# Buffers on multiples of 512 bytes, and half of the later weight buffers 256 bytes off

## The chip, the cores and the metric

The kernel runs on one core of a Trainium2 chip. The metric is the device time of one execution in microseconds, the median of several runs. A core has TensorE for matrix products (each a load of a stationary operand of up to 128 columns, and the streaming of a moving operand of up to 512), VectorE, ScalarE and GpSimd for elementwise work, and queues that start DMAs; on-chip memory has 128 partitions, and "bytes" below are bytes within a partition.

## What is computed

Two blocks, one after the other, on 512 tokens of 1024 features in float32:

```python
def reference(x, ...):
    # first block: h = rmsnorm(x); proj = h @ w_in; three mixers; w_out; residual; gated feed-forward
    x = first_block(x, ...)
    # second block, two layers: even_mixer or odd_mixer, then a feed-forward with a causal convolution
    return second_block(x, ...)

def first_block(...):
    ...
    mix = jnp.concatenate([att, ssd, gdn], axis=-1) @ w_out[l]
    x = x + rmsnorm(mix, post_mix_norm[l])
    h = rmsnorm(x, pre_ffn_norm[l])
    f = (jax.nn.silu(h @ ffn_w_gate[l]) * (h @ ffn_w_up[l])) @ ffn_w_down[l]
    x = x + rmsnorm(f, post_ffn_norm[l])

def second_block(...):
    for layer in range(DEPTH_2):
        m = even_mixer(...) if layer % 2 == 0 else odd_mixer(...)
        x = layer_norm(ALPHA * x + m, ln_g[layer, 0], ln_b[layer, 0])
        f = conv_ffn(x, ffn_w_up[layer], ffn_conv_w[layer], ffn_w_down[layer])
        x = layer_norm(ALPHA * x + f, ln_g[layer, 1], ln_b[layer, 1])
```

The feed-forwards are 2816 wide. Most of the arithmetic is in the products with weights: the projections of three mixers, their output products, and three feed-forwards.

## The kernel before

Products with weights are done to nearly float32 precision from parts: each operand is split exactly into a high and a low part (`split`, lines 327 to 330: ScalarE casts to the high part, VectorE subtracts for the low part; float32r is the type of the parts), and three products are summed in one PSUM bank, high with high, high with low, low with high.

There are two forms. `fm` (lines 350 to 352) makes a block of 128 output features for all tokens: the weights (128 columns, 512 bytes) are loaded, and the activations (512 tokens, 2048 bytes) are the moving operand; eight k-tiles of three products are 24 matmuls. `fm_first` (line 354) does the first blocks behind a tail in two halves of 256 tokens. `tm_k` (lines 364 to 366), called from `tm`, from `out_proj` and from `down` in `ffn`, makes a token tile: the activations (128 tokens, 512 bytes) are loaded and the weights (192 to 512 columns) are the moving operand.

The phases run one after the other: `block1_mix`, output product (`wo1`), feed-forward (`wf1`), `even_mix`, `wo2`, `wf2`, `odd_mix`, `wo3`, `wf3`. A feed-forward makes 11 hidden tiles (22 blocks of `fm`), multiplies them down (`down`), makes 11 more, multiplies seven down, and does the last four token tile by token tile with the tail (`Tail`: residual, norms, transposes, the next operand).

Weights come through `Stream.next` (line 224): 128 x 1024 floats from SyncE's queue into a raw buffer, split into a high and a low one. The pool `const` has two raw buffers and three of each part; between `wo1` and `wf1`, and again from `wo2` to the end, a second pool `w` of the same size is open (`more_weights`), and buffers are taken from the two in turn. The activations of products have two homes: A (`half_act("A")`, in the pool `const`) holds a mixer's output, a feed-forward's hidden tiles 0 to 7 of eleven and block 1's input; B (in the pool `x`, at the right end of the memory, with the residual stream) holds the input of the feed-forwards and of the later mixers. Hidden tiles 8 to 10 are in `hid`.

A pool gives its tiles addresses in the order of their first allocation, each rounded up to 32 bytes. `const` begins at 16,512 (a multiple of 512 and 128 more) with `cst` (5224 bytes), `vecs` (256), `rows` (2512), `eps6` and `eps5` (4 each); A, the raw buffers and the weight parts follow, all multiples of 4096. Pool `w` begins where `const` ends, the pool of a phase where `w` ends. `x` ends at 229,344 and is 49,152 bytes long. Adding up gives where the operands of the products begin, in bytes past a multiple of 512 (each later k-tile, half or token tile in them lies whole multiples of 512 further):

| operand | before | after |
|---|---|---|
| A | 32 | 0 |
| weights in `const` | 32 | 0 |
| weights in `w`, `wo1` and `wf1` | 32 | 0 |
| weights in `w`, `wo2` to `wf3` | 32 | 256 |
| B | 480 | 0 |
| `hid` in `wf1` | 160 | 0 |
| `hid` in `wf2` and `wf3` | 192 | 256 |

Two small tiles matter below: `strictr`, loaded by the products of L508 and L509 in block 1, and their moving operand `tda`, both at 352.

Of the kernel before, what the change touches and what calls it, by code (L numbers as in the profile page):

```python
# [26 lines left out]
# ---------------------------------------------------------------- host layout  # L27

def _fm(w, cols=None):
    """Columns in blocks of 128, each block as [k-row, k-tile, column]."""  # L30
    w = np.asarray(w)
    if cols is not None:
        out = np.zeros((w.shape[0], len(cols)), w.dtype)
        cols = np.asarray(cols)
        out[:, cols >= 0] = w[:, cols[cols >= 0]]
        w = out
    k, c = w.shape
    return w.reshape(k // 128, 128, c // 128, 128).transpose(1, 2, 0, 3).reshape(128, -1)


def _tm(w, cols=None, rows=None):
    """[k-row, k-tile, column] of a group of columns."""
    w = np.asarray(w)
    if cols is not None:
        w = w[:, np.asarray(cols)]
    if rows is not None:
        w = w[np.asarray(rows)]
    k, c = w.shape
    return w.reshape(k // 128, 128, c).transpose(1, 0, 2).reshape(128, -1)
# [18 lines left out]
def _vec(w):  # L68
    """[c] or [n, c] to [128, c/128 * n], channel on the partition."""
# [53 lines left out]
def _t5_onehot():  # L123
    """Column m holds the bucket of distance 255 - m."""
# [7 lines left out]
# packed rows that every partition holds  # L132
# [8 lines left out]
# packed vectors with the channel on the partition  # L141
# [7 lines left out]
# columns of w_in, and how its rows and those of w_out are placed  # L149
# [66 lines left out]
# ---------------------------------------------------------------- kernel  # L216

class Stream:
    """Weights in the order of their use: loaded ahead and split exactly, w = hi + lo. The buffers that stay for
    the whole kernel take turns with those of k.wpool, where that is open."""  # L220
# [4 lines left out]
    def next(self, n, tail=False):  # L225
        """tail: needed at the end of a tail, when VectorE is the busiest."""
# [14 lines left out]
class Kern:  # L241
    def __init__(self, tc, ctx, io):
# [9 lines left out]
        self.eps5 = self.cpool.tile([128, 1], F32, name="eps5")  # L252
        nc.gpsimd.memset(self.eps5, 1e-5)
        self.ident = self.c("ident")
        self.wpool, self.wturn = None, 0
        self.banks = ctx.enter_context(tc.tile_pool(name="banks", bufs=1, space=PSUM))

    def more_weights(self):
        """Further buffers for the weights, over several phases."""
# [14 lines left out]
    def rings(self, **r):  # L274
        """Rings of PSUM banks, for this phase."""
# [36 lines left out]
    # ---- the activations of the next product, feature on the partition, split as hi + lo  # L312

    def open_x(self, ctx):
        """The residual stream, and the second set of operands."""
# [3 lines left out]
    def half_act(self, which, g, dt=F32R):  # L319
        pool = self.cpool if which == "A" else self.xpool  # L320
        return tuple(pool.tile([128, 4, T], dt, name=f"act{p}{g}", bufs=1) for p in "hl")

    def new_act(self, which):
        """A mixer's output is in A, the residual stream as an operand in B (in A before the first mixer)."""
        return {g: self.half_act(which, g) for g in range(2)}

    def split(self, hi, lo, src, eng=None):
        """hi + lo = src, exactly."""
# [3 lines left out]
    def put_act(self, a, t, src, ring):  # L332
        """src: token tile t [128, D], token on the partition."""
# [11 lines left out]
    def fm(self, ps, w, act, nk=KD, s=slice(0, T)):  # L345
        """ps [128, T] = (block of 128 columns)^T act, for the tokens s."""
# [7 lines left out]
    def fm_first(self, ws, act, n, ring, tail):  # L354
        """The first n blocks after a tail: the first two token tiles of each, then the others."""
# [12 lines left out]
    def tm(self, w, act, n, ring, use, ts=range(NT)):  # L368
        """use(t, ps): token tile t of a group of n columns, token on the partition."""
# [8 lines left out]
    def rsqrt(self, out, ss, scale, eps, pool):  # L378
        """(ss * scale + eps) ** -0.5 by Newton's steps on VectorE (ScalarE's tables stay as they are)."""
# [14 lines left out]
def block1_mix(k):  # L394
    """Pre-norm, projections and the three mixers. Returns what w_out multiplies."""
# [3 lines left out]
    # what lives to the end  # L399
# [12 lines left out]
    # pre-norm  # L412
# [16 lines left out]
    def silu2(out, ps):  # L429
        """2 silu"""  # L430
# [3 lines left out]
    # ---- the small projections, attention's v, the delta rule's gate (token on the partition)  # L434
# [11 lines left out]
    def bc(ap, n):  # L446
        """[128, a, b] against [128, a, b, n]."""
# [5 lines left out]
    # gates: da = -exp(A_log) softplus(x + bias) for the four delta heads and the eight of the state space  # L453
# [46 lines left out]
    def decay_ps(mask, t, h0, tag):  # L500
        """[s, 4, t]: the sum of da over s < k <= t."""
# [10 lines left out]
    # the decays within the chunks: for the systems (strict, times -beta) and for the queries  # L512
# [12 lines left out]
    # ---- gated delta rule: q, k, v  # L525
# [4 lines left out]
    def conv(out, ps, wname, b, bias):  # L530
        """silu of the causal convolution of four taps over the tokens; the taps and the bias are halved,
        and silu(2 y) = y (1 + tanh(y))."""
# [23 lines left out]
    # normalised q, k  # L556
# [19 lines left out]
    def chunk_stage(t):  # L576
# [17 lines left out]
        for i, dst in enumerate((gA, gQK)):  # L594
# [4 lines left out]
            if i == 0:  # L599
                # the diagonal blocks of 16, by column  # L600
# [12 lines left out]
    # the unit triangular blocks of 16, one per partition: inverses by substitution  # L613
# [23 lines left out]
    # right-hand sides  # L637
# [9 lines left out]
    # ---- state space: B, C, x, then its gate  # L647
# [5 lines left out]
    # ---- banded attention with sinks  # L653
# [108 lines left out]
    # blocks of 16 to blocks of 32, then the solution of each chunk: above and below the diagonal block of 32  # L762
# [58 lines left out]
    # the chunks' maps of the state, S -> A S + B, and what the state gives to the outputs  # L821
# [27 lines left out]
    # the recurrence over chunks of 64 tokens; the states of two heads on the diagonal of one tile  # L849
# [40 lines left out]
    # what w_out multiplies: state space, delta rule, attention; the norms of the first three token tiles together  # L890
# [14 lines left out]
    for ts in (range(3), range(3, NT)):  # L905
# [6 lines left out]
        # of the doubled gates: half of them, over the root of a quarter of their mean square  # L912
# [11 lines left out]
def softplus(k, pool, out, x, bias, shape):  # L924
    """max(x, 0) + log1p(exp(-|x|)), of x + bias; log1p(e) = 2 atanh(e / (2 + e)) by its series."""
# [24 lines left out]
class Tail:  # L950
    """Residual and norms at the end of a branch, token tile by token tile, up to the next product's operand."""

    def __init__(self, k, pool, kind, i, j, ring):
        """kind "rms": x += rmsnorm(y) * gain i, then rmsnorm * gain j (None: x as it is);
        "ln": x = layernorm(y) * gain i + gain j, y with the residual already in it."""
# [7 lines left out]
    def table(self):  # L963
        """Sqrt's table, before it is waited for."""
# [10 lines left out]
    def part(self, t, c, ps, acc=None):  # L975
        """Half c of the branch's output for token tile t, or the first part of its sum."""
# [7 lines left out]
    def more(self, t, c, ps):  # L984
        """A further part of the sum."""
# [3 lines left out]
    def last(self, t, c, ps, more):  # L989
        """The last part of half c (or all of it), with its statistics."""  # L990
# [17 lines left out]
    def tile(self, t, out=None):  # L1008
        """The rest, once both halves are there."""
# [7 lines left out]
        else:  # L1017
            # minus the mean, then the squares of what is left
# [36 lines left out]
def out_proj(k, ws, act, tail, order):  # L1055
    """The product at the end of a mixer (eight k-tiles), with its tail. Rings "y" of four banks, "z" of two."""
# [26 lines left out]
def ffn(k, wname, act, cvec, kind, gi, gj, out=None):  # L1083
    """The gated feed-forward, plain or (cvec) with its causal convolution of three taps; its tail."""
# [3 lines left out]
    with tc.tile_pool(name=wname, bufs=1, reuse_waits="tile") as P:  # L1088
        k.rings(h=(0, 1, 2, 3), y=(4, 5, 6, 7), bt=(0, 1))
        ws = Stream(k, k.io[wname])  # L1090
        tail = Tail(k, P, kind, gi, gj, "bt")
        taps = None if cvec is None else k.load_vec(cvec, P)
        ha = k.new_act("A")
        hp = P.tile([128, 2, 3, T], F32R, name="hid", bufs=1)
# [60 lines left out]
def even_mix(k, act):  # L1155
    """The even mixer: indexed latent attention and forgetting attention."""
# [26 lines left out]
    # t5 bias of the tokens up to 255 behind a query, by head: a Toeplitz tile from a row, first upside down  # L1183
# [6 lines left out]
    brow = tile_([8, 384], "brow")  # L1190
# [7 lines left out]
    # the index: queries, key, head weights; the forget gates  # L1198
# [288 lines left out]
```

## Time and profile before

| | us |
|---|---|
| median of 3 runs | 1941.91 (1941.82 to 1942.63) |
| span of the profiled execution | 1938.9 |
| TensorE busy with matmuls | 1896.9 (98%) |
| TensorE's weight loads, beside the matmuls | 1554.8 (80%) |
| VectorE busy | 1068.7 (55%) |
| ScalarE busy | 726.9 (37%) |
| GpSimd busy | 158.2 (8%) |

The span runs from the first to the last instruction; the times of the runs contain what lies around it too. Matmuls overlap in the profile, and their ends are modelled; the distance from the start of one to the start of the next is what one costs in a dense stretch. The rows come from the page of the profile, the chain of work that ended last, the waits of TensorE, the groups of instructions by shape, the windows (busy time, count of instructions, granted clock of a stretch) and the timeline (instructions in order of time).

### The profile page before, as it was taken

To read this page: it belongs to the slowest core of one execution; us is meant where nothing else is said; L and a number is where in the kernel's file an instruction comes from. 1 tells how busy PE (TensorE), PEld (TensorE's weight loads), DVE (VectorE), ACT (ScalarE), POOL (GpSimd) and SP (SyncE) were. 2 spreads that over 40 slices of the span, in tenths; PEclk is the share of its full clock that TensorE was granted. 3 is DMA by queue.
4 is the path that set the end of the run, shared out by engine and by line. 5 is a ranking of instruction groups with operands and counts; after the bars stand their busy time and mean duration, and the time that the engine had idled before them with its cause. 6 is when DMAs were issued, how large, how long until landed. Compare 5 with 4: busy or idle time off the path is not lost.

```text
span 1938.9 us, 24632 instructions
## 1 busy us (share of the span) xinstructions
PE 1896.9 (98%) x9635; PEld 1554.8 (80%) x9635; DVE 1068.7 (55%) x2062; ACT 726.9 (37%) x1250; POOL 158.2 (8%) x168
## 2 busy tenths in 40 slices
PE   6999999999999999999999999999999999999998
PEld 6889868888888887776779888888898888888886
DVE  7878775332233365883456643564674376525655
ACT  4534344322222243345544332332433253313332
POOL 1403202000000010011220000000210010000000
PEclk9999999999999999999999999999999999999999
DMA  5221033332332233220033323322332333233321
GB/s 169 87 72 34 23 104 125 109 93 82 109 98 88 72 86 118 66 86 13 1 119 122 98 78 108 98 86 88 104 99 84 102 121 98 83 102 98 93 82 44
DMA packets 50133, 171.54 MB, mean 88 GB/s; under 512 B 5912, under 2 KB 7520, under 8 KB 49760
## 3 DMA queue, kind: packets, MB, share of 16 engines
q1 hardware_dynamic: 46848, 161.71, 27.6%
q10 hardware_dynamic: 3168, 8.25, 1.3%
q8 instruction: 76, 1.25, 0.3%
q14 instruction: 41, 0.34, 0.1%
HBM read 167.81 MB, written 2.13 MB: 88 GB/s over the span
## 4 chain that ended last, share of the span: by engine, by line
PE 94%; DVE 3%; ACT 1%; issue 1%; DMA 1%; POOL 0%; SPq 0%; DVEq 0%; ACTq 0%
PE bank L351 17%; PE bank L350 17%; PE bank L352 17%; PE bank L364 10%; PE bank L365 10%; PE bank L366 10%; PE bank L1298 2%; PE bank L1313 2%; PE bank L341 1%; PE bank L1309 1%; PE bank L777 1%; DVE wlo L330 1%; DMA wraw<-in_w_dram 1%; PE bank L1263 0%; DVE actl L330 0%
## 5 line engine op out<-in xcount | busy, mean ns | idle before, releaser
L330 DVE TENSOR_TENSOR wlo<-wraw,whi 128x1024 fp32r<-128x1024 f32 (+3 forms) x279 | 340.0, 1220 | 467.2 <-ACT whi L329 458.4
L351 PE MATMUL bank<-actl,whi 128*128 128x512 f32 (+1 forms) x1552 | 588.0, 379 | 5.0 <-DVE actl L330 5.0
L352 PE MATMUL bank<-acth,wlo 128*128 128x512 f32 (+1 forms) x1552 | 587.0, 379 | 1.9 <-DVE wlo L330 1.9
L350 PE MATMUL bank<-acth,whi 128*128 128x512 f32 (+1 forms) x1552 | 586.4, 380 | 1.0 <-DVE actl L1205 0.3
L329 ACT CAST whi<-wraw 128x1024 fp32r<-128x1024 f32 (+3 forms) x295 | 303.1, 1029 | 629.3 <-PE bank L351 341.7
L351 PEld LDWEIGHTS bank<-actl,whi 128*128 128x128 f32 x1552 | 293.9, 189 | 64.1 <-DVE actl L330 5.5
L352 PEld LDWEIGHTS bank<-acth,wlo 128*128 128x128 f32 x1552 | 293.9, 189 | 60.9 <-DVE wlo L330 2.1
L350 PEld LDWEIGHTS bank<-acth,whi 128*128 128x128 f32 x1552 | 292.3, 189 | 62.3 <-issue 1.8
L364 PE MATMUL bank<-whi,acth 128*128 128x512 f32 (+3 forms) x896 | 316.6, 355 | 2.7 <-ACT acth L329 1.8
L365 PE MATMUL bank<-wlo,acth 128*128 128x512 f32 (+3 forms) x896 | 316.0, 353 | 0.1
L366 PE MATMUL bank<-whi,actl 128*128 128x512 f32 (+3 forms) x896 | 315.2, 353 | 0.0
L364 PEld LDWEIGHTS bank<-whi,acth 128*128 128x128 f32 x896 | 169.9, 190 | 30.0 <-ACT acth L329 2.5
L365 PEld LDWEIGHTS bank<-wlo,acth 128*128 128x128 f32 x896 | 169.9, 190 | 24.1 <-issue 1.0
L366 PEld LDWEIGHTS bank<-whi,actl 128*128 128x128 f32 x896 | 169.8, 190 | 24.0 <-issue 1.0
L330 POOL TENSOR_TENSOR wlo<-wraw,whi 128x1024 fp32r<-128x1024 f32 x16 | 39.4, 2475 | 592.2 <-ACT whi L329 589.1
L1101 DVE SCALAR_TENSOR_TENSOR cv<-bank,fcw,cv 128x510 f32<-128x510 f32 x88 | 65.8, 748 | 2.8
L1100 DVE SCALAR_TENSOR_TENSOR cv<-bank,fcw,cv 128x511 f32<-128x511 f32 x88 | 65.5, 744 | 0.0
L1117 ACT ACTIVATE cv<-cv 128x512 f32<-128x512 f32 x44 | 27.8, 632 | 90.8 <-DVE cv L1101 90.8
L330 DVE TENSOR_TENSOR actl<-bank,acth 128x512 fp32r<-128x512 f32 (+1 forms) x68 | 44.2, 669 | 30.1 <-ACT acth L329 29.8
L329 ACT CAST acth<-cv 128x512 fp32r<-128x512 f32 x48 | 29.7, 620 | 80.9 <-DVE cv L1118 80.5
L1099 ACT ACTIVATE cv<-bank,fcw 128x512 f32<-128x512 f32 x88 | 60.0, 681 | 0.0
L365 PE MATMUL bank<-wlo,hid 128*128 128x512 f32 x144 | 57.3, 398 | 0.0
(380 smaller groups left out, 1852.2 us busy)
## 6 DMA issues: line engine op xcount, KB each, us to landing
wraw<-in_wf_dram SPq DMA_DIRECT2D x192, 512.0 KB, 3.5
wraw<-in_w_dram SPq DMA_DIRECT2D x63, 512.0 KB, 3.7
wraw<-in_wo_dram SPq DMA_DIRECT2D x24, 512.0 KB, 3.6
gain<-in_gains_dram ACTq DMA_DIRECT2D x12, 512.0 KB, 4.3
wraw<-in_wf_dram SPq DMA_DIRECT2D x12, 256.0 KB, 2.7
xt<-in_x_dram SPq DMA_DIRECT2D x4, 512.0 KB, 5.3
x<-in_x_dram SPq DMA_DIRECT2D x4, 512.0 KB, 6.1
out_dram<-x SPq DMA_DIRECT2D x8, 256.0 KB, 2.0
```

Of the source, the lines that this page charges most:

```text
L329: self.nc.scalar.copy(hi, src)
L330: (eng or self.nc.vector).tensor_tensor(lo, src, hi.bitcast(F32), op=ALU.subtract)
L350: self.nc.tensor.matmul(ps[:, s], hi[:, k, :], ah, start=(k == 0), stop=False)
L351: self.nc.tensor.matmul(ps[:, s], hi[:, k, :], al, start=False, stop=False)
L352: self.nc.tensor.matmul(ps[:, s], lo[:, k, :], ah, start=False, stop=(k == nk - 1))
L364: self.nc.tensor.matmul(ps, ah, wh, start=first, stop=False)
L365: self.nc.tensor.matmul(ps, ah, wl, start=False, stop=False)
L366: self.nc.tensor.matmul(ps, al, wh, start=False, stop=last)
L1099: S.activation(o, ps, AF.Copy, scale=w(2))
L1100: V.scalar_tensor_tensor(o[:, 1:], ps[:, :T - 1], w(1), o[:, 1:], op0=ALU.mult, op1=ALU.add)
L1101: V.scalar_tensor_tensor(o[:, 2:], ps[:, :T - 2], w(0), o[:, 2:], op0=ALU.mult, op1=ALU.add)
L1298: E.matmul(p, q_[h // 2][q, tok(t)], k_[h // 2][q, :n], start=True, stop=True)
```

## The change

- `eps5`, which nothing reads, is no longer allocated, so A and the weights of `const` move down by 32 bytes.
- A tile `xend` of 480 bytes, which nothing reads, is allocated behind B, so that `x` and B begin 480 bytes further down.
- A tile `wline` of 256 bytes, which nothing reads, is allocated first in the pool `w` that is open from `wo2` on.
- In `ffn`, `hid` (and A, which has its place already) is allocated ahead of the tail's tiles, and so lies at the start of the phase's pool; the tail's gains and sums lie behind it.
- In `even_mix`, `brow` takes a slot of the ring `pT` in place of a tile of its own.

Comments and docstrings are removed as well. No operation on data is added or removed but the memset of `eps5`.

```diff
         nc.gpsimd.memset(self.eps6, 1e-6)
-        self.eps5 = self.cpool.tile([128, 1], F32, name="eps5")
-        nc.gpsimd.memset(self.eps5, 1e-5)
         self.ident = self.c("ident")
-        self.wpool, self.wturn = None, 0
+        self.wpool, self.wturn, self.xend = None, 0, None
...
     def half_act(self, which, g, dt=F32R):
         pool = self.cpool if which == "A" else self.xpool
-        return tuple(pool.tile([128, 4, T], dt, name=f"act{p}{g}", bufs=1) for p in "hl")
+        t = tuple(pool.tile([128, 4, T], dt, name=f"act{p}{g}", bufs=1) for p in "hl")
+        if which == "B" and g == 1 and self.xend is None:
+            self.xend = pool.tile([128, 120], F32, name="xend")
+        return t
...
         ws = Stream(k, k.io[wname])
+        ha = k.new_act("A")
+        hp = P.tile([128, 2, 3, T], F32R, name="hid", bufs=1)
         tail = Tail(k, P, kind, gi, gj, "bt")
         taps = None if cvec is None else k.load_vec(cvec, P)
-        ha = k.new_act("A")
-        hp = P.tile([128, 2, 3, T], F32R, name="hid", bufs=1)
...
-    brow = tile_([8, 384], "brow")
+    brow = tile_([128, 512], "pT", 4)[0:8, 0:384]
...
     act = even_mix(k, act)
     with k.more_weights() as k.wpool:
+        k.wpool.tile([128, 64], F32, name="wline")
         act = project("wo2", act, "ln", 4, 8)
```

## Rows read from the trace of the kernel before

**Rows 1.** The page: its first line, and its busy time by engine.
```profile
span 1938.9 us, 24632 instructions
PE 1896.9 (98%) x9635; PEld 1554.8 (80%) x9635; DVE 1068.7 (55%) x2062; ACT 726.9 (37%) x1250; POOL 158.2 (8%) x168
```
**Rows 2.** The chain that ended last: shares by engine, then by line.
```profile
PE 94%; DVE 3%; ACT 1%; issue 1%; DMA 1%; POOL 0%; SPq 0%; DVEq 0%; ACTq 0%
PE bank L351 17%; PE bank L350 17%; PE bank L352 17%; PE bank L364 10%; PE bank L365 10%; PE bank L366 10%; PE bank L1298 2%; PE bank L1313 2%; PE bank L341 1%; PE bank L1309 1%; PE bank L777 1%; DVE wlo L330 1%; DMA wraw<-in_w_dram 1%; PE bank L1263 0%; DVE actl L330 0%
```
**Rows 3.** Waits of TensorE, longest first: total us, times, longest.
```profile
PE bank L341 <- DMA wraw<-in_w_dram: 12.9, 1, 12.9
PE bank L351 <- DVE actl L330: 5.0, 2, 2.7
```
**Rows 4.** Timeline (start, us, engine, line): first `fm` product of `wf1`, product behind 432.
```profile
353.19 0.39 PE L350 MATMUL bank<-acth,whi 128*128 128x512 f32 x1
...
453.98 0.40 PE L364 MATMUL bank<-whi,acth 128*128 128x512 f32 x1
```
**Rows 5.** Timeline of `down` in `wf2`: first product, after 96, after 36 more.
```profile
1143.36 0.40 PE L364 MATMUL bank<-whi,acth 128*128 128x512 f32 x1
...
1165.15 0.39 PE L364 MATMUL bank<-whi,hid 128*128 128x512 f32 x1
...
1173.55 0.40 PE L364 MATMUL bank<-whi,acth 128*128 128x512 f32 x1
```
**Rows 6.** Window in `fm` of `wf1`: length, TensorE busy (count), granted clock, DMA.
```profile
360.00:440.00 80.00, 80.00 (x345) 1.00 0.30 89
```
**Rows 7.** Groups of matmuls by line and shape: count, busy us, mean ns, idle before.
```profile
L350 PE MATMUL bank<-acth,whi 128*128 128x512 f32 x1312 | 520.2, 396 | 0.5 <-DVE actl L1205 0.3
...
L364 PE MATMUL bank<-whi,acth 128*128 128x512 f32 x576 | 224.1, 391 | 0.9 <-ACT acth L329 0.6 <-ACT whi L329 0.3
...
L364 PE MATMUL bank<-whi,acth 128*128 128x256 f32 x256 | 74.2, 291 | 0.5 <-DVE actl L330 0.5
...
L350 PE MATMUL bank<-acth,whi 128*128 128x256 f32 x240 | 66.2, 288 | 0.5 <-DVE actl L330 0.3
...
L364 PE MATMUL bank<-whi,hid 128*128 128x512 f32 x144 | 56.9, 395 | 0.0
```
**Rows 8.** Timeline of `fm` in block 1, with L508 in between.
```profile
60.01 0.39 PE L350 MATMUL bank<-acth,whi 128*128 128x512 f32 x1
...
61.37 0.39 PE L350 MATMUL bank<-acth,whi 128*128 128x512 f32 x1
61.59 0.40 PE L508 MATMUL bank<-tda,strictr 128*128 128x512 f32 x1
61.83 0.39 PE L351 MATMUL bank<-actl,whi 128*128 128x512 f32 x1
```
**Rows 9.** Timeline of `fm_first` in `wf2`: first product, and the one behind 114.
```profile
1029.54 0.37 PE L350 MATMUL bank<-acth,whi 128*128 128x256 f32 x1
...
1042.57 0.39 PE L350 MATMUL bank<-acth,whi 128*128 128x512 f32 x1
```
**Rows 10.** Timeline of `tm` in `odd_mix`: two starts, ten products apart.
```profile
1419.81 0.28 PE L365 MATMUL bank<-wlo,acth 128*128 128x256 f32 x1
...
1420.99 0.28 PE L366 MATMUL bank<-whi,actl 128*128 128x256 f32 x1
```
**Rows 11.** Timeline of `tm` in block 1: two starts, 14 products apart.
```profile
167.73 0.28 PE L366 MATMUL bank<-whi,actl 128*128 128x256 f32 x1
...
169.41 0.28 PE L365 MATMUL bank<-wlo,acth 128*128 128x256 f32 x1
```
**Rows 12.** Timeline of ScalarE at the start of `wf1`, behind the tail of `wo1`.
```profile
341.58 0.33 ACTq L309 DMA_DIRECT2D gain<-in_gains_dram  x1
342.06 0.21 ACT L965 ACTIVATE tsq<-eps 128x1 f32<-128x1 f32 x1
```
**Rows 13.** The tile `gain`: its DMAs from issue to landing.
```profile
DMA to landing us min/median/max: 3.7/4.1/7.2
```

## The prediction

> **What bounds the kernel now.** First the page: TensorE's matmuls cover 98% of the span, VectorE 55%, ScalarE 37% [rows 1]. Busy shares of TensorE are modelled, so next the chain that ended last: 94% of the span is TensorE, and its three largest lines are the three products of `fm` (51% together), then the three of `tm_k` (about 30%) [rows 2]. Then TensorE's waits: the longest is one of 12.9 us at the start, the next 5.0 us [rows 3]. So there is no idle time to win; what a change can win is the time of one product, and the reader has to look at the distance from one start to the next, not at the recorded 0.39 us, which overlap.
>
> That distance isn't the same for equal shapes. In the first feed-forward 432 products of `fm`, 512 columns each, start at 353.19 and the first product behind them at 453.98: 100.79 / 432 = 233.3 ns [rows 4]. In `down`, 96 products of the same size, now with weights as the moving operand and an A operand as the loaded one, go from 1143.36 to 1165.15: 227.0 ns; the 36 behind them differ only in that the loaded operand is a `hid` tile: 8.40 / 36 = 233.3 ns [rows 5]. One column per cycle at 2.4 GHz would be 213.3 ns, and the granted clock is at that level, 1.00, within the first of these stretches [rows 6]. So each product loses 14 to 20 ns to something other than the clock, and how much goes with the operands. The table in the section on the kernel gives their places: the fast pair begins 32 bytes past a multiple of 512 on both sides; B operands begin at 480, `hid` at 160 or 192.
>
> **Part 1, the moving operand of `fm` from 480 to 0.** Lines 350 to 352 run 3 x 1312 products of 512 columns [rows 7]; 17 blocks of 24 are in block 1 and take A, which leaves 3936 - 408 = 3528 with B. No row has a full-rate product that begins at 0. The nearest is the start at 32: block 1's `fm`, the same code with A at 32, goes from 60.01 to 61.37 in six products, 227 ns [rows 8]. There too the product just ahead of L508 takes 0.22 us while a tile at 352 is being loaded, and L508 itself, moving from 352, takes 0.24 us while weights at 32 are loaded: the start of the moving operand matters more than that of the loaded one. I take 227: 3528 x (233.3 - 227.0) = 22.2 us won. Bounds: nothing, if place and not alignment makes the difference (B lies at the far end of the memory, A at its front), and 3528 x 20 = 70.6 us at one column per cycle.
>
> **Part 2, products of 256 columns.** `fm_first` has 3 x 240 of these [rows 7]; with B at 480 they take 13.03 / 114 = 114 ns [rows 9]. Products of 256 columns whose moving operand begins at 32 take longer: 1.18 / 10 = 118 ns with the loaded operand at 480 [rows 10], 1.68 / 14 = 120 ns with both at 32 [rows 11]. So the start that is best for 512 columns is not best for 256. With the row nearest to equal starts: 720 x 6 = 4.3 us lost, and 576 of the 768 in `tm` (the 192 of block 1 stay as they are) x 2 = 1.2 us. Bounds: 720 x (114 - 106.7) + 576 x (118 - 106.7) = 11.8 us won at one column per cycle, 5.5 us lost. I take 5.5 lost.
>
> **Part 3, `tm` and `hid`.** 1728 products of `tm_k` with 512 columns load an A operand and 432 a `hid` tile [rows 7]. A and the weights go from 32 and 32 to 0 and 0: equal starts as before, taken at no gain (bound: 1728 x 13.7 = 23.7 us at one column per cycle). `hid` in the first feed-forward goes from 160 to 0: 144 x 6.3 = 0.9 us. In the two later ones it goes to 256, and equals the weights in every second buffer only: half of 288 x 6.3 = 0.9 us, between 0 and 1.8.
>
> **Part 4, every second weight buffer at 256 in the later phases.** For `tm` this takes the moving operand away from an equal start: 1152 products of that kind lie there (two feed-forwards with 384, two output products with 192), half use the shifted buffers. Between no cost and the level of unequal starts, 576 x 6.3 = 3.6 us; I take half, 1.8 us lost. For `fm` only the loaded operand is shifted: by [rows 8] that costs nothing, bound 1104 x 6.3 = 7.0 us.
>
> **Part 5, the rest.** `hid` is now allocated ahead of the tail's gains and sums, so the gain's DMA, which ScalarE issues, waits for other tiles of the phase before: in the first feed-forward for the third tile of the old sums, whose last reader is its transposes. That DMA is issued at 341.58, behind the last split of the operand, by when those transposes are done; behind it on ScalarE's queue stands a table load at 342.06 [rows 12], which nothing needs before the end of the feed-forward. If it did hold the queue, the price would be one wait of about the 4.1 us that a gain takes to land [rows 13], once in a feed-forward. `brow` as a slot of `pT`: written and sent at the start of its phase, ahead of all the index work; the first attention, which takes the other slots first, comes after that, so no cost. `xend` and `wline` are never read. The memset that goes with `eps5` lies under TensorE's wait of 12.9 us at the start [rows 3].
>
> **Sum.** 22.2 + 0.9 + 0.9 - 5.5 - 1.8 = 16.7 us, of which I count the chain's 94% [rows 2]: 16 us. The profiled execution's span is 1938.9 [rows 1] and the median 1941.9, so 3.0 us lie around it and stay. 1941.9 - 16 = 1926 us.
>
> **The rule that speaks against it.** The rows show equal shapes at 227 and 233 ns [rows 4, 5]. The Trainium skill, "SBUF — State Buffer", section "Who interferes with whom", gives TensorE two independent read ports and says that it never waits on anyone, and its section "Operand start alignment" asks for multiples of the element size alone, adding that this is about legality, not speed. By that the sum is nought. The two paces of the rows disagree with the first rule taken strictly, though they can't say whether alignment or place is behind them.
> Its page "TensorE: Matmul & The Clock Gate", section "Back-to-back issue gap", has columns over 2.4 GHz plus some 2.5 ns for an isolated product. No row at full rate reaches that (215.8 ns at 512 columns); with it in all products the sum would be about 90 us, an estimate.
>
> **Rivals.**
> *It does less than it says: place, not alignment.* B at the far end, `hid` in the middle and A at the front are confounded with their offsets in nearly all rows. For it: `hid` and B both take 233.3 ns at different offsets. Against: L508, moving from neither end, and the slow product behind a fast one [rows 8]. Then parts 1 to 4 are nought: 1942 us.
> *Aligned starts remove most of the loss.* If it comes from runs of 512 bytes that straddle a boundary, a start at 0 is another case than one at 32, and the loss falls to the 6 to 7 ns that 256 columns show today [rows 9] over 106.7: 220 ns. Then 3528 x 13.3 + 432 x 13.3 + (1728 + 408) x 7 = 68 us, with 94% 64: 1878 us. For it: nothing measured here lies on a multiple of 64, and the excess of 20 ns is large. Against: 32 is only one step from 0 and has most of 14 ns left.
> *Slower: equal starts collide.* Where loading and streaming run side by side all the time, at 256 columns, equal starts are the slowest (120 against 118 and 114 ns) [rows 9 to 11]. If exact alignment does that to 512 columns too, the products with equal starts (1320 of `fm` up to the middle of the kernel, half of the 2208 behind it) take 6 ns more instead of less: 2424 x 6 = 14.5 us and part 2's 5.5 us, 19 us with 94%: 1961 us. It decides where a product of `fm` in the first feed-forward takes over 233.3 ns. Against: at 512 columns equal starts are the fastest today [rows 5].
>
> **How the numbers follow.** The forecast, 0.43: 1926, between 1920 and 1936 by its own bounds. Most of the loss removed, 0.25: 1878, down to 1855 with 256 columns and `tm` better too. Nought, 0.15. Slower, 0.17. About 0.2%, some 4 us, is what a measurement of this kernel can tell from no change; the forecast and the second case lie beyond it on the fast side: faster 0.68, same 0.15, slower 0.17. Leaving out under one in ten at either end, the range is 1855 to 1953.
>
> **What would show it.** In the profile after, the first feed-forward's 432 products of `fm` divide the sum: 227 ns for the forecast (98 us), 220 or less for the second case (95 us), 233 for place, over 236 for collisions. The next `fm_first` should take about 120 ns a product. In the later feed-forwards the pace of `fm` should be the same in blocks with either buffer; if it alternates, part 4 is wrong. `down` should stay at 227 in the first feed-forward. A new wait of TensorE at the start of a feed-forward would point to part 5. The forecast is wrong if the pace of `fm` doesn't change, or if `tm`, which I hold constant, moves by more than 2 ns: its 1728 products are worth 3.5 us for it.

## Result: 15 us faster, by the product of 512 columns

| | before | after |
|---|---|---|
| median of 5 runs beside each other, us | 1941.91 (1939.23 to 1942.63) | 1926.94 (1919.74 to 1933.99) |
| ratio, 95% interval | | 0.992 [0.9892, 0.9947] |
| span of the profiled execution, us | 1938.9 | 1932.2 |
| mean granted clock of that execution | 0.993 | 0.985 |

The forecast was 1926 us, between 1855 and 1953. In the code of after `fm` has lines 352 to 354 and `tm_k` 366 to 368. First the page: its first line and the busy time by engine, as in [rows 1].

```profile
span 1932.2 us, 24631 instructions
PE 1890.2 (98%) x9635; PEld 1571.9 (81%) x9635; DVE 1069.2 (55%) x2062; ACT 727.0 (38%) x1250; POOL 157.6 (8%) x167
```

The instructions are the same but for one memset less on GpSimd; only the time of each can have changed. The timeline of TensorE after (start, us, engine, line, operation) shows where, at the places of [rows 4] and of `down` behind it: the first product of `fm` in `wf1`, the product behind 432 of them, the one behind 96 of `tm` that load A, the one behind 36 that load `hid`.

```profile
366.31 0.40 PE L352 MATMUL bank<-acth,whi 128*128 128x512 f32 x1
...
464.26 0.39 PE L366 MATMUL bank<-whi,acth 128*128 128x512 f32 x1
...
486.02 0.39 PE L366 MATMUL bank<-whi,hid 128*128 128x512 f32 x1
...
494.18 0.39 PE L366 MATMUL bank<-whi,acth 128*128 128x512 f32 x1
```

97.95 / 432, 21.76 / 96 and 8.16 / 36 are all 226.7 ns; before it was 233.3 in `fm` [rows 4] and 227.0 and 233.3 in `down` of `wf2` [rows 5]. The 256-column products went the other way. `fm_first` of `wf2`, the rows that answer to [rows 9]:

```profile
1035.20 0.36 PE L352 MATMUL bank<-acth,whi 128*128 128x256 f32 x1
...
1048.96 0.40 PE L352 MATMUL bank<-acth,whi 128*128 128x512 f32 x1
```

13.76 / 114 = 120.7 ns; before it was 114.3.

The profiled execution gains only 6.7 us, and the windows say why (length, TensorE busy and count, granted clock, share of the DMA engines, GB/s). After: from the first `fm` of block 1 to the first full-width `fm` of `wf1`, then from there to the end, then a piece of block 1.

```profile
32.64:366.31 333.67, 327.43 (x2002) 0.94 0.23 73
366.31:1932.20 1565.89, 1544.81 (x7509) 0.99 0.30 90
155.80:176.30 20.50, 20.50 (x94) 0.50 0.02 7
```

The same windows of before, by its own landmarks:

```profile
32.79:353.19 320.40, 314.15 (x2003) 0.98 0.24 76
353.19:1938.90 1585.71, 1564.82 (x7509) 0.99 0.30 89
155.80:176.30 20.50, 20.27 (x164) 1.00 0.17 53
```

From `wf1` on, at a clock of 0.99 in both, the change gains 1585.71 - 1565.89 = 19.8 us. Ahead of it this execution loses 13.3 us, with the clock at 0.94 instead of 0.98: for 20.5 us of block 1 it was granted 0.50, the lower level of 1.2 GHz, and 94 products ran there instead of 164. That isn't the change: the kernel `wline128` (below), the changed one but for 128 bytes in a pool that opens only behind `even_mix`, passed the same stretch at 0.98 in 321.65 us, and `b_only` (below), in which all but B lies where it lay before, was granted 0.50 from 155.80 to 176.30 as well, with 94 products.

```profile
33.00:354.65 321.65, 315.29 (x2002) 0.98 0.24 76
```

The five runs of after carry mean clocks of 0.985 to 0.993, and their times go with it: 1933.99 and 1932.68 at 0.985, 1926.94 at 0.988, 1921.37 at 0.992, 1919.74 at 0.993. Before at 0.993 takes 1938.95 to 1940.49 in the runs beside the experiments. At equal clocks the change is worth about 20 us, 1.0%; the ratio of the medians has less of it, since the median run of after was at 0.988 (the clocks of the five runs of before aren't on record; 1941.91 is what before took at 0.991 to 0.992 beside the experiments).

### The profile page after: what moved, and what is told of

It is laid out like the page before. It is cut to its first block, busy times and chain, and to the rows that moved or that the text cites. A ratio compares the mean times of both kernels' runs of the same rounds, so it can differ in the third digit from the quotient of the medians.

```text
span 1932.2 us, 24631 instructions
## 1 busy us (share of the span) xinstructions
PE 1890.2 (98%) x9635; PEld 1571.9 (81%) x9635; DVE 1069.2 (55%) x2062; ACT 727.0 (38%) x1250; POOL 157.6 (8%) x167
## 4 chain that ended last, share of the span: by engine, by line
PE 95%; DVE 2%; ACT 1%; issue 1%; DMA 1%; POOL 0%; SPq 0%; DVEq 0%; ACTq 0%
PE bank L353 17%; PE bank L354 17%; PE bank L352 17%; PE bank L366 10%; PE bank L367 10%; PE bank L368 10%; PE bank L1300 2%; PE bank L1315 2%; PE bank L343 1%; PE bank L779 1%; PE bank L1311 1%; DVE wlo L332 1%; DMA wraw<-in_w_dram 1%; PE bank L1265 0%; ACT whi L331 0%
## 5 line engine op out<-in xcount | busy, mean ns | idle before, releaser
L366 PE MATMUL bank<-whi,acth 128*128 128x512 f32 (+3 forms) x896 | 321.0, 360 | 2.8 <-ACT acth L331 1.7
L367 PE MATMUL bank<-wlo,acth 128*128 128x512 f32 (+3 forms) x896 | 320.3, 358 | 0.1
L368 PE MATMUL bank<-whi,actl 128*128 128x512 f32 (+3 forms) x896 | 319.5, 358 | 0.0
L366 PEld LDWEIGHTS bank<-whi,acth 128*128 128x128 f32 x896 | 174.5, 195 | 29.7 <-ACT acth L331 2.4
L367 PEld LDWEIGHTS bank<-wlo,acth 128*128 128x128 f32 x896 | 174.6, 195 | 24.1 <-issue 1.0
L368 PEld LDWEIGHTS bank<-whi,actl 128*128 128x128 f32 x896 | 174.3, 195 | 23.7 <-issue 1.2
L368 PE MATMUL bank<-whi,hid 128*128 128x512 f32 x144 | 56.3, 391 | 0.0
```

The lines of the kernel that those rows point to most:

```text
L366: self.nc.tensor.matmul(ps, ah, wh, start=first, stop=False)
L367: self.nc.tensor.matmul(ps, ah, wl, start=False, stop=False)
L368: self.nc.tensor.matmul(ps, al, wh, start=False, stop=last)
```

## The experiments

Three theories. Theory 1 is the prediction's: where the moving operand begins decides the pace of a product of 512 columns, the loaded one's start hardly matters. Theory 2: the two starts of one product have to be equal, modulo some number of bytes; absolute places don't count. Theory 3: the place in the memory decides (B at its far end), the starts don't. The first four kernels:

**`b_only`**: of the change only what moves B, from 480 to 0; weights and A stay at 32, `hid` where it was.

```diff
+        if which == "B" and g == 1 and self.xend is None:
+            self.xend = pool.tile([128, 120], F32, name="xend")
...
+    brow = tile_([128, 512], "pT", 4)[0:8, 0:384]
```

> The kernel before with one part alone: the 480 bytes behind B (and brow in a slot of pT, which makes room), so B begins at 0 and everything else stays: weights and A at 32, hid at 160 and 192. Theory 1, the start of the operands decides, each for itself: fm with 512 columns takes 226.7 ns as in the changed kernel, hid stays at 233, products of 256 columns in fm_first take 120 in place of 114 ns; 3528 x 6.6 less and 720 x 6 more, about 1923 us at the clock of before. Theory 2, what counts is that both operands begin at the same place modulo 512: B at 0 and weights at 32 differ, fm stays at 233 ns, 1942 us. Theory 3, the place in the memory decides: 1942 us as well, B lies where it lay.

Measured: 1947.21 us (12 runs) beside 1944.62 of before (23 runs), ratio 1.0017 [0.9993, 1.0041]. Its timeline of TensorE, first the 432 products of `fm` in `wf1` and the product behind them, then 114 of `fm_first` in `wf2` and the product behind those:

```profile
365.29 0.40 PE L353 MATMUL bank<-acth,whi 128*128 128x512 f32 x1
...
466.08 0.40 PE L367 MATMUL bank<-whi,acth 128*128 128x512 f32 x1
...
1043.72 0.37 PE L353 MATMUL bank<-acth,whi 128*128 128x256 f32 x1
...
1057.29 0.40 PE L353 MATMUL bank<-acth,whi 128*128 128x512 f32 x1
```

100.79 / 432 = 233.3 ns: `fm` doesn't gain a nanosecond from a moving operand that begins at 0. `fm_first` loses, 13.57 / 114 = 119.0 ns against 114.3. Theory 1 is false.

**`no_xend`**: the change without `xend`, so that B stays at 480 and all else is moved.

```diff
-            self.xend = pool.tile([128, 120], F32, name="xend")
+            self.xend = self
```

> The changed kernel without the 480 bytes behind B, so B begins at 480 again; weights, A and hid at 0 or 256 as in the changed kernel. Theory 1: fm with 512 columns at 233.3 ns, fm_first at 114 ns, hid at 226.7 (432 x 6.6 = 2.9 us less than before): about 1939 us. If the start of the weights helps the products of fm too, their pace is below 233 and the time below 1935 us. Theory 3: 1942 us with hid at 233 ns.

Measured: 1940.80 us (12 runs), ratio 0.9998 [0.9969, 1.0027]. In its timeline `fm` of `wf1` keeps 100.80 / 432 = 233.3 ns, while `hid` (36 products from 477.25) takes 8.16 / 36 = 226.7:

```profile
354.68 0.40 PE L352 MATMUL bank<-acth,whi 128*128 128x512 f32 x1
...
455.48 0.40 PE L366 MATMUL bank<-whi,acth 128*128 128x512 f32 x1
...
477.25 0.39 PE L366 MATMUL bank<-whi,hid 128*128 128x512 f32 x1
...
485.41 0.39 PE L366 MATMUL bank<-whi,acth 128*128 128x512 f32 x1
```

`fm_first` of `wf2` takes 119.1 ns (114 products from 1031.67 to 1045.25), where theory 1 expected 114; that loss eats up what `hid` gains. Neither moving B alone nor moving the rest alone gives `fm` anything; the gain needs both. And the two kernels agree at both widths, 233.3 and 119 ns, with other starts but the same difference: 0 less 32 and 480 less 0 are both 224 modulo 256. That speaks for theory 2.

**`no_wline`**: the change without `wline`, so that all weight buffers and `hid` begin at 0.

```diff
-        k.wpool.tile([128, 64], F32, name="wline")
```

> The changed kernel without the 256 bytes ahead of the later weight buffers: all operands of products begin at 0. Theory 1, with the changed kernel's 226.7 ns at 0 and at 256 alike: every product of 512 columns at 226.7 ns, the time that of the changed kernel within 2 us when the granted clock is the same. If the 256 bytes were good for something, TensorE's products or the splits of the weights in the phases from wo2 on take longer than in the changed kernel, by more than 3 us in sum. The granted clock decides the rest: 0.985 to 0.993 in five executions of the changed kernel went with 1934 to 1920 us.

Measured: 1923.28 us (6 runs), ratio 0.9905 [0.9872, 0.9938]. The products of 512 columns in all three feed-forwards take 226.7 ns, `fm_first` of `wf2` 120.7, as in the change. The 256 bytes do nothing that can be measured.

**`micro`**: the change, and behind its output products of 512 and 256 columns, eight to a group, with the loaded operand at 0, 32, 160 and 256 and the moving one at 0, 32 and so on up to 480; no other engine works there.

```diff
+        for n in (512, 256):
+            for st in (0, 32, 160, 256):
+                for i in range(17):
+                    o, s = (0 if i == 16 else i * 8), (sa, sb)[i % 2]
...
+                        nc.tensor.matmul(ps, s[:, st // 4:st // 4 + 128], mv[:, o:o + n], start=True, stop=True)
```

> The changed kernel with 1088 products more behind its output, which measure the pace by itself: 8 for each start of the moving operand (0 to 480 in steps of 32, and 0 again) and of the loaded one (0, 32, 160, 256), first with 512 and then with 256 columns; no other engine works then. Theory 1: with 512 columns 226.7 ns at moving starts of 0, 32 and 256, and 232 to 233.5 at 352 and 480, more with a load from 160; with 256 columns 120 ns at 0 and 114 at 480. Theory 2: 226.7 only where both starts are equal. Theory 3: no start makes a difference within these three tiles. If the 13 ns over one column per cycle come from the other engines' traffic, the pace here is nearer to 213.3 ns. About 190 us more than the changed kernel.

Measured: in its timeline, first a group with the loaded operand at 0 and the moving one at 32, and the row behind it; then one with both at 32, and the row behind that:

```profile
1918.21 2.03 PE L1458 MATMUL bank<-mv,sb 128*128 128x512 f32 x8
1920.08 2.00 PE L1458 MATMUL bank<-mv,sa 128*128 128x512 f32 x8
...
1949.85 1.98 PE L1458 MATMUL bank<-mv,sb 128*128 128x512 f32 x8
1951.67 2.03 PE L1458 MATMUL bank<-mv,sa 128*128 128x512 f32 x8
```

1.87 / 8 = 233.8 and 1.82 / 8 = 227.5 ns, with the same moving operand. Of all groups, the mean distance of starts in the later five products, worked out from the timeline; the column is the moving start less the loaded one, modulo 256, and each cell holds eight to ten groups with different absolute starts:

```
difference    0         32     64     96     128    160    192    224
512 columns   226.6-231 233.8  228.8  234.6  234.1  233.8  233.3  232.5   ns
256 columns   119.2     118.5  117.7  118.0  118.8  117.3  113.5  117.5   ns
```

Nearly all groups of a cell lie within 0.4 ns of each other, whichever absolute starts make the difference; only at a difference of 0 do groups of eight at 512 columns scatter (longer ones, below, come to 226.7). So the difference counts and 256 bytes is its period, which is why `wline` does nothing. And since no other engine worked (in 180 us of it VectorE is busy for 0.3 us, ScalarE and GpSimd for none, the DMA engines for 1%), the loss is TensorE's own, not a neighbour's traffic.

**`equal32`**: back to the kernel before, and everything brought to 32 past a multiple of 256: B by a tile of 448 bytes behind it, `hid` by allocating it first (`brow` makes room as in `b_only`). Nothing begins on a multiple of 512.

```diff
...
+            self.xend = pool.tile([128, 112], F32, name="xend")
...
+        ha = k.new_act("A")
+        hp = P.tile([128, 2, 3, T], F32R, name="hid", bufs=1)
         tail = Tail(k, P, kind, gi, gj, "bt")
         taps = None if cvec is None else k.load_vec(cvec, P)
-        ha = k.new_act("A")
-        hp = P.tile([128, 2, 3, T], F32R, name="hid", bufs=1)
...
```

> The kernel before, with B and `hid` moved so that everything begins 32 bytes past a multiple of 256: weights, A, B (a tile of 448 bytes behind it) and `hid` (allocated first). Nothing begins on a multiple of 512. Theory 2 (what counts is the difference of the two starts, modulo 256): every product of 512 columns takes 226.7 ns, `fm_first` 119.9 instead of 113.4, and the whole is as fast as the change: 3528 x 6.6 of `fm` and 432 x 6.6 of `hid` won, 720 x 6.4 and 576 x 1.8 of the 256-column products lost, 20 us in all, ratio 0.990. Rival (multiples of 512 count, as the change's name says): `fm` stays at 233.3 ns and the time at the kernel before's.

Measured: 1924.55 us (6 runs), ratio 0.9896 [0.9863, 0.9929]. `fm` of `wf1` in its timeline:

```profile
354.27 0.40 PE L353 MATMUL bank<-acth,whi 128*128 128x512 f32 x1
...
452.22 0.39 PE L367 MATMUL bank<-whi,acth 128*128 128x512 f32 x1
```

97.95 / 432 = 226.7 ns, `hid` 226.7 and `fm_first` 120.7 as well. It has the whole gain with no operand on a multiple of 512: the multiples of 512 that the change aims at are one way to equal starts and nothing else.

**`wline128`**: the changed kernel with 128 bytes in place of the 256 of `wline`.

```diff
-        k.wpool.tile([128, 64], F32, name="wline")
+        k.wpool.tile([128, 32], F32, name="wline")
```

> The changed kernel with a `wline` of 128 bytes instead of 256, so that half of the later weight buffers, and the later `hid`, begin at 128 past a multiple of 256 and all else at 0. Theory 2 with period 256: in the later feed-forwards the pace of `fm` alternates, 226.7 ns in blocks with an unshifted buffer and 233.3 with a shifted one; `tm` likewise; the first feed-forward keeps 226.7. 1104 of `fm`, 576 of `tm` and 144 of `hid` lose 6.6 ns: 12 us more than the change, near 1939. Rival (only the moving operand's start counts, the loaded one's doesn't): `fm` keeps 226.7 with either buffer, `tm` alternates, 4 to 5 us more. Rival (period 512, or nothing: shifts of the weights don't show, as 256 bytes didn't): no alternation, the time of the change.

Measured: 1936.52 us (10 runs), ratio 0.9956 [0.993, 0.9983], 12 us above `equal32` on the same chip. The first products of four blocks of `fm` in `wf2`, 24 products apart, whose weights begin at 0, 128, 0 and 128 by turns:

```profile
1039.43 0.40 PE L352 MATMUL bank<-acth,whi 128*128 128x512 f32 x1
...
1044.89 0.40 PE L352 MATMUL bank<-acth,whi 128*128 128x512 f32 x1
...
1050.48 0.39 PE L352 MATMUL bank<-acth,whi 128*128 128x512 f32 x1
...
1055.93 0.40 PE L352 MATMUL bank<-acth,whi 128*128 128x512 f32 x1
```

5.46, 5.59 and 5.45 us: 227.5, 232.9 and 227.1 ns, block by block in one execution, with the moving operand the same. `wf1`, where no buffer is shifted, keeps 226.7. The loaded operand's start counts as much as the moving one's, and 12 us is what was expected over a kernel with equal starts.

**`micro2`**: the change, and behind its output groups of 24: finer starts, fewer loaded columns, other widths.

```diff
+        for o in range(0, 288, 8):
+            group(512, 0, o, 128, 24)
+        for c in (128, 64, 32):
+            for o in (0, 64, 96, 192):
+                group(512, 0, o, c, 24)
+        for n in (128, 256, 384):
+            for o in (0, 64, 128, 192):
+                group(n, 0, o, 128, 24)
```

> The changed kernel with dense products behind its output, in groups of 24 that alternate between two loaded tiles; no other engine works there. First 512 columns, loaded operand at 0, moving one at 0, 8, 16 up to 280 bytes. If the memory gives out its rows in pieces of 32 or 64 bytes, the pace goes in steps of four or eight starts; if each column counts, 8 is as slow as 32; both have 256 to 280 like 0 to 24. Then 128, 64 and 32 loaded columns at differences of 0, 64, 96 and 192 bytes. If the loss over 213.3 ns comes from loading beside streaming, it shrinks with the columns loaded: 13.4 and 20 ns at 128 to about 3.4 and 5 at 32. If it is the moving operand's own, it stays at 13.4 and the difference of the starts still counts. Last 128, 256 and 384 columns at differences of 0, 64, 128 and 192: a loss per load would be the same number of ns at each width, a loss per column would be in proportion to the width.

Its timeline shows a group as one row; the distance to the next row over 24 is the pace (tiles `sa` and `sb` take turns as the loaded one). Rows of the first part, for differences of 8 and 16, and of 256, 264 and 272; then 32 loaded columns at differences of 0, 64 and 96.

```profile
1923.56 5.77 PE L1457 MATMUL bank<-mv,sb 128*128 128x512 f32 x24
1929.17 5.72 PE L1457 MATMUL bank<-mv,sa 128*128 128x512 f32 x24
...
2097.00 5.63 PE L1457 MATMUL bank<-mv,sa 128*128 128x512 f32 x24
2102.46 5.77 PE L1457 MATMUL bank<-mv,sb 128*128 128x512 f32 x24
2108.07 5.72 PE L1457 MATMUL bank<-mv,sa 128*128 128x512 f32 x24
...
2163.55 5.71 PE L1457 MATMUL bank<-mv,sa 128*32 128x512 f32 x24
2169.10 5.72 PE L1457 MATMUL bank<-mv,sb 128*32 128x512 f32 x24
2174.66 5.76 PE L1457 MATMUL bank<-mv,sa 128*32 128x512 f32 x24
```

A difference of 8 bytes already costs all: 5.61 / 24 = 233.8 ns; at 256 it is 5.46 / 24 = 227.5 (226.7 over the later half of the group), at 264 233.8 again. In the later half of their groups the other differences take 228.6 ns (at 64) to 240.0 (at 120), with no steps of 32 or 64 bytes, and 264 to 280 repeat 8 to 24 within 0.2 ns. With 32 loaded columns the pace is 231.3 ns at a difference of 0 and 231.7 at 64: it doesn't shrink with the columns loaded, as it should if the loss were one of so many columns loaded beside the stream; but equal starts win next to nothing there. By width, at equal starts, the later half of each group takes 120.0, 173.3 and 226.7 ns for 256, 384 and 512 columns, which is 13.3 ns above a column per cycle of 2.4 GHz at each: a cost per product, not per column. That isn't the whole of it: 128 columns take 111.5 to 111.9 ns at all four differences, 58 above, and 384 columns take 173.4 at differences of 64 and 192 too, and 175.8 at 128, so that equal starts win little at that width.

**`micro3`**: groups of 32 again, now two products by turns whose operands begin at 0 and at a difference; then more widths, more places for 256 columns, and bfloat16.

```diff
+            for d in (64, 128, 192):
+                group(n, [(sa, 0, mv, 0), (sb, d, mw, d)], 32)
+                group(n, [(sa, 0, mw, d), (sb, d, mv, 0)], 32)
...
+        for d in (0, 64, 128, 192):
+            group(512, [(sz, 0, mz, d)], 32, 2)
```

> The changed kernel with dense products behind its output, 32 to a group. First, at 512 and at 256 columns, two products take turns. In one kind of group each product's moving operand is at an equal start with its own loaded operand and at a difference of 64, 128 or 192 bytes from that of the product behind it; in the other kind it is the reverse. Theory 2a (the loss arises where the moving operand of one product streams beside the loading of the next one's operand): at 512 columns the first kind takes 229 to 233.3 ns and the second 226.7; at 256 columns the first 114 to 118.5 and the second 120. Theory 2b (a product's own two operands count): the other way round. Then widths of 320 and 448 columns at differences of 0, 128 and 192. If equal starts cost 13.3 ns at any width and unequal ones 6.7 ns per 128 columns beyond the first, 320 columns take 146.7 and 143.3 ns, 448 columns 200 and 203.3. If the loss is in proportion to the width, 141.7 at equal starts with 320 columns. Then 256 columns at a difference of 192 from several starts, with one product repeated or three in the order of `fm`: 113.4 as in the kernel before if the start alone decides, up to 118 if the order or the place has a part in it. Last 512 columns of bfloat16 at differences of 0, 64, 128 and 192: 226.7 and up to 233.3 if the rule is one of product and load, equal paces below 226.7 if it is one of operands of 4 bytes.

Its timeline at 512 columns: the first products of three groups, and the row of the bfloat16 groups. In the first (from 1939.29) a product is equal with its own loaded operand and 64 off from the next one's; in the second it is the reverse.

```profile
1939.29 0.39 PE L1459 MATMUL bank<-mv,sa 128*128 128x512 f32 x1
...
1946.69 0.40 PE L1459 MATMUL bank<-mw,sa 128*128 128x512 f32 x1
...
1954.16 0.39 PE L1459 MATMUL bank<-mv,sa 128*128 128x512 f32 x1
...
2081.21 27.80 PE L1459 MATMUL bank<-mz,sz 128*128 128x512 bf16 x125
```

7.40 / 32 = 231.3 and 7.47 / 32 = 233.4 ns; for 128 it is 228.6 and 230.0, for 192 231.9 and 233.0. Neither kind keeps 226.7, so neither of the expected forms holds: it isn't the own pair of starts alone, nor the moving operand against the next load alone. At 256 columns the second kind has the 120 ns of equal starts at 64 and 192 (and the first 117), as theory 2a has it, but at 128 both take 117. The mechanism stays open. The bfloat16 group, in its last row, is one row for all four differences: 128 products (the trace has 125 of them) in 27.42 us from the first start to the last, 127 distances of 215.9 ns. So bfloat16 products don't show the rule at these differences. Whether that is their two bytes or their quicker load isn't told apart: in this trace a load of 128 columns takes 98 ns in bfloat16 and 188 in four bytes.

The widths falsify the form that was guessed for unequal starts. 320 columns take 146.7 ns at differences of 0, 128 and 192, where 143.3 was expected at the latter two; 448 take 202.7, 203.8 and 202.2, where 200 and 203.3 were expected. And 256 columns at a difference of 192 take 113.3 ns from three pairs of starts (32 and 224, 32 and 480, 0 and 448) and 117.8 from two others (0 and 192, 64 and 256), with one product repeated or in the order of `fm` alike; in `micro` the same difference gave 113.5 at all eight pairs. What else counts at 256 columns is open.

## Why the prediction was right, and which steps of it were not

The time was right to a microsecond, by luck in part; that the products of 512 columns give it was right, and the reason why they do wasn't.

**Part 1, the size.** 227 ns was taken for `fm`, and 226.7 came: 3528 x 6.6 = 23.3 us instead of 22.2.

**Part 1, the reason.** The step that failed is the reading of [rows 8]: "the start of the moving operand matters more than that of the loaded one". It rests on two single distances, 0.22 and 0.24 us, read to 0.01 us. `b_only` gave the moving operand its start and got 233.3 ns; `wline128` left it there, moved the loaded one, and got 232.9. The pair to look at stood in the same rows: the fast products began at 32 on both sides, the slow ones at 480 and 32, or 32 and 160 or 192. Nor could the two distances decide it: L508's own two starts are equal, 352 and 352, and its neighbours' are too, and `micro3` shows that products by turns at other starts, each equal with its own, take 228.6 to 231.9 ns. The working came to the right number since the change makes the starts equal as well, and since the row it took the 227 ns from had equal starts.

**Part 2.** `fm_first` lost 114.3 to 120.7 ns, 720 x 6.4 = 4.6 us, for 4.3. `tm` with 256 columns lost somewhat more than the 1.2 us: in `odd_mix` 336 of them go from 41.49 to 42.97 us, 4.4 ns each (123.5 ns before; the ten of [rows 10] with 118 weren't typical), in `even_mix` 48 from 5.76 to 5.86, 2.1 each; with that for the rest, 2 us.

**Part 3.** `tm` with A went from 227.0 to 226.7, as held. `hid` gained in all 432 products, 2.7 us instead of 1.8: a start at 256 is an equal start for weights at 0.

**Part 4.** Nothing was lost (`no_wline`), and `fm` of `wf2` keeps 226.7 ns with either buffer: the 1.8 us fall away for the same reason. The bound of 3.6 for the level of unequal starts was sound: in `wline128`, where half of the starts do differ by 128 bytes, `tm` in the later feed-forwards takes 230.1 ns on the average of both buffers, 3.4 more, and every second block of `fm` 232.9, which is the 7.0 us that the prediction kept as a bound, thought unlikely.

**Part 5.** No wait came at the start of a feed-forward: TensorE's longest waits are of 12.7 us at the start and 5.0 (in two), as before; from `wf1` on TensorE's start distances account for the gain.

**Sum.** 23.3 + 2.7 + 0.5 - 4.6 - 2 = 20 us (0.5 for `tm` with A), where the windows show 19.8 from `wf1` on. The first `fm_first` lies ahead of them, so its 1.5 us of loss aren't in the 19.8, and 1.6 us are missing; they lie at one place, the tail of `wo3`, 16.55 us from 1549.57 after and 14.97 us from 1551.32 before, where the execution of after was granted 0.50 for 3.4 us. The forecast had 16.7, and took 94% of that, a reduction that the windows don't show. That the median agreed with 1926 all the same is luck, by the clock of its runs; at the 0.993 of the profile before it is 1919.74, six below the forecast and just under the 1920 that its own bounds gave.

**The rivals.** Place, not alignment: false, since B never left the far end. Most of the loss removed: false for operands of four bytes, no start gave 512-column products a steady pace below 226.7 ns. (Its two premises were misread: `hid` at 192 does lie on a multiple of 64, and by [rows 9] the loss at 256 columns is 114.3 - 106.7 = 7.6 ns, not 6 to 7.) Equal starts collide: at 256 columns they are the slowest case, as it said, and at 512 the fastest; the row that it named, `fm` of `wf1`, went the other way.

**The rule that spoke against it.** Nothing but the starts of TensorE's own two operands, with every other engine idle, took a 512-column product from 226.7 to 233.3 ns (`micro`, `micro2`). The Trainium skill, "SBUF — State Buffer", section "Who interferes with whom", has TensorE's two read ports independent and never waiting; for four-byte operands the runs speak against that, if it is to say that the two starts don't matter to each other. The Trainium skill's page "TensorE: Matmul & The Clock Gate", section "Back-to-back issue gap", has 2.5 ns on top of the columns for an isolated product; the dense bfloat16 products here come to that (215.9 ns, 2.6 over 213.3), the four-byte ones don't (13.3 over at best at 512 columns, 6.6 at 256).

**Not tried.** A kernel that keeps equal starts for 512 columns and a difference of 192 for `fm_first` alone would win at most its 4.6 us.

## What to carry to other kernels

Read the distance from start to start of equal products and set it beside the starts of both their operands, not of one; with four-byte operands and 128 loaded columns, equal starts modulo 256 bytes were best at 512 columns, worst at 256 and made no difference at 320, and an absolute alignment bought nothing. A reason read from a single product at the clock's last digit wants a count behind it: 432 products in a row told 6.6 ns apart, two of them could not. Compare runs at the same granted clock before a difference of 1% is put down to a change.

## What the runs showed of the hardware

- Dense four-byte products at equal starts cost 13.3 ns each above a column per cycle of 2.4 GHz, the same at 256, 320, 384 and 512 columns (448 had 16.0; 128 columns had 58, at any difference); bfloat16 products of 512 columns cost 2.6. At the lower level of the clock the excess is gone: in the first group of `micro2`, 3 us of which were granted 0.50, the distances are 427 ns, which is 512 columns at 1.2 GHz.
- With 128 loaded columns, the pace of a four-byte product of 512 columns depends on its two starts by their difference modulo 256 bytes: 0 gives 226.7 ns, 64 gives 228.6 to 229, most others 232 to 235; 8 bytes already cost 7 ns. At 256 columns it is the reverse, 120 at 0 and down to 113.3 at 192 (117.8 from some starts). Why isn't shown: two products by turns at mixed starts, and 32 loaded columns instead of 128, fit neither a clash with the next load nor one of the own pair.
- The granted clock of block 1 differs between executions of nearly the same instructions, from 0.94 to 0.98, and with it the length of that stretch, from 320 to 334 us in the traces here. Why it fell to the lower level in one and not in the other isn't shown.
